# An encoder trunk on one core: values of all heads in one Strassen product, ticks kept out of the edge k tiles, and two `w_out` strips made ahead

## The chip, the core and the metric

The kernel runs on one core of one Trainium2 chip. The metric is the device time of one execution in microseconds, as the median of several runs. Engines: PE is TensorE (matrix products; PEld its weight loads), DVE VectorE, ACT ScalarE, POOL GpSimd, SP SyncE, which issues most DMAs. Accumulators lie in eight PSUM banks of 128x512 float32.

## The reference

Two layers on 256 tokens of width 2048, batch 1, float32. In each layer:

```
u = rmsnorm(x) * g
c_q, c_kv, k_pe, q_na, k_na, v_na, gate_a, gate_b = split(u @ w_in)
y_a = latent_attention(c_q, c_kv, k_pe) @ w_o_mla           # 8 heads, low-rank q and kv, rotary key
y_b = neighbourhood_attention(q_na, k_na, v_na) @ w_o_na    # 8 heads of 128, 2-D window, learned bias
x = x + (sigmoid(gate_a) * y_a + sigmoid(gate_b) * y_b) @ w_out
x = x + square(relu(rmsnorm(x) @ w_ff1)) @ w_ff2            # width 8192 in the middle
```

A last RMSNorm follows. Both attentions are softmax over all 256 keys, the second with a window mask.

## The kernel before, in words

**Two halves of a number.** Matmuls take a rounded float32 form (`F32R`). To keep float32 accuracy each operand is split into a rounded part `hi` and a remainder `lo`, and a product is the three matmuls hi·hi, lo·hi and hi·lo. For weights `parts` (line 172) or `weights` (line 180) make the two: ACT casts `hi`, DVE subtracts to get `lo`. Such a pair of tiles is called a strip here. Activations are split in the same way into tiles called `pair`.

**The product helpers.** All of them load weights by a DMA on SP's queue into `raw` (three buffers of 1 MB), make strips in a ring of four, and issue matmuls.
- `gemm_b` (line 347) has weights as the stationary side and gives transposed results in four banks: for each two k tiles 8 matmuls of 512 columns (L354) and 8 of 256 (L359). It makes queries, keys and latents.
- `gemm_a` (line 325, with `group_a` above it) has activations stationary: 12 matmuls of 512 columns for each two k tiles (L306, L310). The values of four heads, `w_o_na` and `w_o_mla` are made so.
- `gemm_s` (line 524) is partly Strassen, over 1024 output columns and row pairs `j` of two k tiles. A plain row pair takes 8 products, that is 24 matmuls; a Strassen pair takes 7, that is 21 (all L537). For a Strassen pair DVE first makes sums of weight blocks (L574 to L578), and the activations need their own sums, called forms (`forms`, line 479). `order` gives the order of the row pairs; in the layer's first half and for `w_out` it is 0, 4, 1, 5, 2, 6, 3, 7, with 1, 2, 3 as Strassen pairs. Before its first Strassen pair `gemm_s` drains all pending small work (`drain`). At its end one copy and eight additions gather the results from eight banks (L586, L587). The gates, `w_out`, `w_ff1` and `w_ff2` use it.

**Small work between products.** Heads, norms, transposes (`turned`) and forms are generators. `tick` (line 128), called by the products between matmuls, advances one of them, or starts a queued head if six ticks have passed; a generator says how many ticks it sleeps. `have` forces work whose result is needed now. In `gemm_b` a tick stands behind every second `hi` matmul. A head (`na_head`, `mla_head`) computes scores, then `softmax_pv` (line 647): maximum, exponential, reciprocal, scaling of the two probability tiles by the reciprocal (L664, on DVE), 13 ticks later the transposes (L669), 3 ticks later the product with the values.

**The order of the program.** The code gives a program order, and a scheduler that simulates the engines moves instructions within each engine; tiles and pools carry the waits. Layer 0 starts with the queries of all eight neighbourhood heads (`gemm_first`), then for each group of four heads: keys, values, and the four heads are queued. In layer 1 each group also makes its queries. Then come the two latent products, the rotary key, gates and `w_o_na`, the eight latent heads, the rest of `w_o_na`, four column blocks of `w_o_mla`, then `w_out`, and the MLP.

**Pools.** The first half of a layer holds strips of 1024 columns in `wpool` and small tiles of the heads in `tmp`; both belong to `half_a`, which closes behind `w_o_mla`. Then `half_b` opens `wpool2` in that space, with strips of 2048 columns (`strips = True`), and `w_out` begins. `slots` is a ring of 51 tiles of 128x512 for activations of all kinds.

Of the kernel before, what the change touches and what calls it, by code (L numbers as in the profile page):

```python
# [33 lines left out]
F32 = mybir.dt.float32  # L34
F32R = mybir.dt.float32r
# [4 lines left out]
P = 128  # L40
# [35 lines left out]
def trunk(ctx: ExitStack, tc: tile.TileContext, x, x_turned, w_in, w_uq, w_ukv, rpb, w_o_mla, w_o_na,  # L76
# [9 lines left out]
    hbufs, smalls, strips = HBUFS, SMALL, False  # L86

    def bank():
        return psum.tile([P, 512], F32, tag="bank", name="bank", bufs=8)
# [82 lines left out]
    def parts(src):  # L172

        lo, hi = (wpool.tile([P, 2048 if strips else 1024], F32R, tag=tag, name=tag,
                             bufs=hbufs)[:, :src.shape[-1]] for tag in ("lo", "hi"))
        nc.scalar.copy(hi, src)  # L176
        nc.vector.tensor_tensor(lo, src, hi.bitcast(F32), op=ALU.subtract)  # L177
        return hi, lo
# [345 lines left out]
    def gemm_s(w, c0, get, order, pairs, evac):  # L524
# [23 lines left out]
        def cut(src):  # L548
            out, step = [], 2048 if strips else 1024
            for c in range(0, src.shape[-1], step):  # L550
                hi, lo = parts(src[:, c:min(c + step, src.shape[-1])])
                out += [(hi[:, i:i + 512], lo[:, i:i + 512]) for i in range(0, hi.shape[-1], 512)]
            return out

        first = next(j for j in order if j in pairs)
        for j in order:
            raw = raws.tile([P, 2048], F32, tag="raw", name="raw", bufs=RBUFS)
            nc.sync.dma_start(raw.rearrange("p (k n) -> p k n", n=1024),
                              w[2 * j * P:(2 * j + 2) * P, c0:c0 + 1024].rearrange("(k p) n -> p k n", p=P))
            if j not in pairs:  # L560
                ws = cut(raw)
# [85 lines left out]
    def softmax_pv(s, scale, vt, j, put):  # L647
# [15 lines left out]
        for b in range(2):  # L663
            nc.vector.tensor_scalar_mul(p[:, b], p[:, b], inv[:, b:b + 1])  # L664
# [87 lines left out]
    for l in range(DEPTH):  # L752
# [3 lines left out]
        tmp = half_a.enter_context(tc.tile_pool(name="tmp", bufs=2, reuse_waits="tile"))  # L756
# [11 lines left out]
        att_na, ke = [None] * HEADS, [None] * 2  # L768
        for g in range(2):
            qn, kn = (qn[4:] if l == 0 and g else [None] * 4), [None] * 4  # L770
            if l == g == 0:
                qn = [None] * 8
                gemm_first(wi, C_QN, xg, xf4, to_pair(None, qn), squared)
                gemm_b(wi, C_KN, xg, to_pair(mix, kn), scaled, weights(wi, NC, C_KN, 512, tc.keep_in_program_order))
                tables()
            else:
                if l == 0:
                    for t in range(2):
                        tc.keep_in_program_order(nc.sync.dma_start(xt[t], x[t * P:(t + 1) * P]))
                else:  # L780
                    gemm_b(wi, C_QN + g * 512, xg, to_pair(None, qn), scaled if g == 0 else None)
                gemm_b(wi, C_KN + g * 512, xg, to_pair(mix, kn))
# [5 lines left out]
            for j in range(4):  # L788
                h = g * 4 + j
                queued.append(na_head(l, h, qn[j], kn[j], vt, mix.query, setter(att_na, h)))  # L790
# [26 lines left out]
        xs4 = [None] * (NC // 2)  # L817
        start(forms(xf4, MIXED, xs4), 10)
# [25 lines left out]
        mixed = blocks(xg, xs4, MIXED)  # L844
# [53 lines left out]
        mg, ms4, mf4 = [None] * NC, [None] * (NC // 2), [None] * (NC // 2)  # L898
        for c4 in range(4):
# [14 lines left out]
        half_b = ExitStack()  # L914
        strips = True
        wpool = half_b.enter_context(tc.tile_pool(name="wpool2", bufs=4, reuse_waits="tile"))
        tmp = half_b.enter_context(tc.tile_pool(name="tmp2", bufs=2, reuse_waits="tile"))
# [12 lines left out]
        for g in range(2):  # L930
# [11 lines left out]
            gemm_s(w_out[l], g * 1024, blocks(mg, ms4, MERGED), ORDER, MERGED, residual)  # L942
# [142 lines left out]
```

## Time and profile before

| | |
|---|---|
| median of 3 runs | 2599.27 us (2599.08 to 2599.73) |
| the profiled execution, own time | 2599.52 us |
| its span, first to last instruction | 2597.7 us |
| PE busy | 2585.0 us, 12432 matmuls |
| DVE busy | 2176.4 us |
| ACT busy | 1487.5 us |
| granted TensorE clock | 0.999 |
| HBM traffic | 494.28 MB read, 2.10 MB written |

A row of a timeline gives the start and the length in microseconds, engine, line, operation, tiles (written <- read), shape and count, and in brackets the idle time ahead and what ended it. Consecutive instructions of one kind are merged. A group's row gives the busy time, the mean duration of one in nanoseconds and the idle time ahead. Matmuls are pipelined: one lasts longer than the distance from one start to the next. In the layer's first half stages of layer 0 lie at: first queries and keys up to 74 us, values of group 0 to 96, keys and values of group 1 to 147, latents and rotary key to 206, first gate to 248, latent heads 397 to 460, `w_o_mla` up to 526, `w_out` from 527.

### The profile page before, as it was taken

To read this page: it belongs to the slowest core of one execution; us is meant where nothing else is said; L and a number is where in the kernel's file an instruction comes from. 1 tells how busy PE (TensorE), PEld (TensorE's weight loads), DVE (VectorE), ACT (ScalarE), POOL (GpSimd) and SP (SyncE) were. 2 spreads that over 40 slices of the span, in tenths; PEclk is the share of its full clock that TensorE was granted. 3 is DMA by queue.
4 is the path that set the end of the run, shared out by engine and by line. 5 is a ranking of instruction groups with operands and counts; after the bars stand their busy time and mean duration, and the time that the engine had idled before them with its cause. 6 is when DMAs were issued, how large, how long until landed. Compare 5 with 4: busy or idle time off the path is not lost.

```text
span 2597.7 us, 32260 instructions
## 1 busy us (share of the span) xinstructions
PE 2585.0 (100%) x12432; PEld 2171.9 (84%) x12432; DVE 2176.4 (84%) x2538; ACT 1487.5 (57%) x1732; POOL 98.0 (4%) x118
## 2 busy tenths in 40 slices
PE   9999999999999999999999999999999999999998
PEld 8888889888888888888888888898888888888887
DVE  7778889699988898888667788896999988988885
ACT  6555557456655645546545555574666556555463
POOL 0200000000000010000001000000000000100000
PEclk9999999999999999999999999999999999999999
DMA  7655564555577585675565555645656765856754
GB/s 266 217 171 195 180 205 151 165 191 195 195 219 220 176 259 198 202 239 171 178 201 178 173 194 182 205 149 161 197 180 211 234 199 192 246 194 209 243 180 145
DMA packets 173994, 511.06 MB, mean 197 GB/s; under 512 B 13840, under 2 KB 18832, under 8 KB 173584
## 3 DMA queue, kind: packets, MB, share of 16 engines
q1 hardware_dynamic: 164640, 491.78, 57.1%
q0 software_dynamic: 8768, 16.78, 3.3%
q8 instruction: 97, 1.59, 0.2%
q10 hardware_dynamic: 432, 0.43, 0.1%
q14 instruction: 57, 0.47, 0.1%
HBM read 494.28 MB, written 2.10 MB: 191 GB/s over the span
## 4 chain that ended last, share of the span: by engine, by line
PE 99%; issue 0%; ACT 0%; DVE 0%; POOL 0%; DVEq 0%; POOLq 0%; ACTq 0%
PE bank L537 67%; PE bank L306 8%; PE bank L354 6%; PE bank L310 4%; PE bank L359 3%; PE bank L285 2%; PE bank L507 1%; PE bank L260 1%; PE bank L286 1%; PE bank L314 1%; PE bank L316 1%; PE bank L315 1%; PE bank L258 1%; PE bank L669 1%; PE bank L605 0%
## 5 line engine op out<-in xcount | busy, mean ns | idle before, releaser
L537 PE MATMUL bank<-hi,pair 128*128 128x512 f32 x5124 | 1283.4, 390 | 2.1 <-ACT hi L176 2.1
L537 PEld LDWEIGHTS bank<-hi,pair 128*128 128x128 f32 x5124 | 958.0, 188 | 202.5 <-ACT hi L176 2.9
L176 ACT CAST hi<-raw 128x2048 fp32r<-128x2048 f32 (+3 forms) x416 | 622.7, 1517 | 301.7 <-PE bank L537 165.3
L177 DVE TENSOR_TENSOR lo<-raw,hi 128x2048 fp32r<-128x2048 f32 (+3 forms) x416 | 741.6, 1796 | 63.8 <-ACT hi L176 42.2
L537 PE MATMUL bank<-lo,pair 128*128 128x512 f32 x2562 | 697.2, 390 | 0.0
L537 PEld LDWEIGHTS bank<-lo,pair 128*128 128x128 f32 x2562 | 479.7, 188 | 99.4
L176 ACT CAST hi<-sums 128x2048 fp32r<-128x2048 f32 (+1 forms) x150 | 244.9, 1638 | 297.5 <-DVE sums L578 168.9
L177 DVE TENSOR_TENSOR lo<-sums,hi 128x2048 fp32r<-128x2048 f32 (+1 forms) x150 | 290.7, 1948 | 101.2 <-ACT hi L176 58.2
L198 DVE TENSOR_TENSOR lo<-raw,hi 128x1024 fp32r<-128x1024 f32 (+1 forms) x208 | 248.8, 1201 | 102.9 <-ACT hi L197 99.5
L197 ACT CAST hi<-raw 128x1024 fp32r<-128x1024 f32 (+1 forms) x208 | 214.1, 1035 | 205.0 <-PE bank L306 87.6
L306 PE MATMUL bank<-hi,pair 128*128 128x512 f32 x960 | 245.2, 392 | 0.0
L586 DVE TENSOR_TENSOR wide<-wide,bank 128x512 f32<-128x512 f32 x336 | 214.9, 679 | 6.5 <-PE bank L537 6.4
L306 PEld LDWEIGHTS bank<-hi,pair 128*128 128x128 f32 x960 | 178.3, 188 | 35.8
L354 PE MATMUL bank<-pair,hi 128*128 128x512 f32 x640 | 168.8, 395 | 0.0
L574 DVE TENSOR_TENSOR sums<-raw 128x1024 f32<-128x1024 f32 x126 | 153.7, 1220 | 13.9 <-DMA raw<-in_w_ff 7.3
L310 PE MATMUL bank<-lo,pair 128*128 128x512 f32 x480 | 131.9, 391 | 0.0
L354 PEld LDWEIGHTS bank<-pair,hi 128*128 128x128 f32 x640 | 112.4, 189 | 17.7
L310 PEld LDWEIGHTS bank<-lo,pair 128*128 128x128 f32 x480 | 89.4, 188 | 18.0
L516 ACT CAST pair<-wide 128x512 fp32r<-128x512 f32 x110 | 68.2, 620 | 59.8 <-DVE wide L475 57.5
L359 PEld LDWEIGHTS bank<-pair,lo 128*128 128x128 f32 x640 | 89.4, 190 | 7.2
L359 PE MATMUL bank<-pair,lo 128*128 128x256 f32 x640 | 93.7, 283 | 0.0
L578 DVE TENSOR_TENSOR sums<-raw,sums 128x512 f32<-128x512 f32 x126 | 86.6, 687 | 2.0
(165 smaller groups left out, 1890.7 us busy)
## 6 DMA issues: line engine op xcount, KB each, us to landing
raw<-in_w_ff SPq DMA_DIRECT2D x256, 1024.0 KB, 5.4
raw<-in_w_in SPq DMA_DIRECT2D x120, 1024.0 KB, 5.1
raw<-in_w_out SPq DMA_DIRECT2D x32, 1024.0 KB, 5.6
raw<-in_w_o_na SPq DMA_DIRECT2D x16, 1024.0 KB, 5.0
raw<-in_w_o_mla SPq DMA_DIRECT2D x16, 1024.0 KB, 5.0
xt<-wide POOLq DMA_DIRECT2D x48, 256.0 KB, 5.3
raw<-in_w_in SPq DMA_DIRECT2D x17, 512.0 KB, 5.6
raw<-in_w_ukv SPq DMA_DIRECT2D x8, 1024.0 KB, 5.0
```

The lines of the kernel that those rows point to most:

```text
L176: nc.scalar.copy(hi, src)
L177: nc.vector.tensor_tensor(lo, src, hi.bitcast(F32), op=ALU.subtract)
L197: nc.scalar.copy(hi, src)
L198: nc.vector.tensor_tensor(lo, src, hi.bitcast(F32), op=ALU.subtract)
L306: nc.tensor.matmul(ps[t], a, wh[:, k], start=k0 + k + i == 0, stop=False)
L310: nc.tensor.matmul(ps[t], sides(have(acts, k0 + k), t)[0], wl[:, k], start=False, stop=k0 + k == nk - 1)
L354: nc.tensor.matmul(ps[m], wh[:, k, m * P:(m + 1) * P], have(acts, k0 + k), start=k0 + k == 0, stop=False)
L359: nc.tensor.matmul(ps[m][:, :S], wl[:, k, m * P:(m + 1) * P], have(acts, k0 + k)[:, :S], start=False, stop=k0 + k == nk - 1)
L537: nc.tensor.matmul(b[i], x, y, start=count[i] == 1, stop=count[i] == total[i])
L574: nc.vector.tensor_tensor(ts[0].rearrange("p (a n) -> p a n", a=2), raw[:, :512].rearrange("p (a n) -> p a n", a=1).to_broadcast([P, 2, 512]),
L578: final = nc.vector.tensor_tensor(t4, raw[:, 1536:], t2, op=ALU.subtract)
L586: add = lambda o, a, c: nc.vector.tensor_tensor(o, a, c, op=ALU.add)
```

## The change

Five edits.

1. **Values.** One `gemm_s` over all 1024 value columns takes the place of two products of `gemm_a`'s kind (issued in the main body by `group_a`). The forms of x, made so far during the first latent product, are made ahead of it. The results reach `values` from gathered tiles instead of from banks. The first four heads are queued behind it.
2. **Ticks.** `gemm_b` calls no tick in the first two and the last two k tiles.
3. **Softmax scaling** goes from DVE to ACT.
4. **Strips ahead.** During the last column block of `w_o_mla`, a generator closes `tmp`, opens a pool `wpool3` in its space and makes the strips of `w_out`'s row pairs 0 and 4 there. `gemm_s` takes them from `made`. Strips of 2048 columns now alternate, two and two, between `wpool3` and `wpool2` with two buffers each.
5. **Order.** Each such strip's cast and subtraction may not pass the previous strip's on its engine (a dependency without a semaphore).

```diff
@@ parts
+        if strips:
+            whole_strips[0] += 1
+        pool, n, bufs = (stores[whole_strips[0] // 2 % 2], 2048, 2) if strips else (wpool, 1024, HBUFS)
...
+        if strips:
+            for ins, last in zip(made, previous):
+                tc.add_manual_dep(ins.ins, last, ...)
+            previous[:] = [ins.ins.name for ins in made]
@@ gemm_b
-                    if m % 2:
+                    if m % 2 and 0 < k0 < nk - 2:
                         tick()
@@ gemm_s
-            raw = raws.tile([P, 2048], F32, tag="raw", name="raw", bufs=RBUFS)
-            nc.sync.dma_start(...)
+            raw = None if j in made else two_rows(w, c0, j)
             if j not in pairs:
-                ws = cut(raw)
+                ws = made[j] if j in made else cut(raw)
@@ softmax_pv
-            nc.vector.tensor_scalar_mul(p[:, b], p[:, b], inv[:, b:b + 1])
+            nc.scalar.activation(p[:, b], p[:, b], AF.Copy, scale=inv[:, b:b + 1])
@@ main body, first half of a layer
+        if l == 0:
+            gemm_first(wi, C_QN, xg, xf4, to_pair(None, qn), squared)
+            start(forms(xf4, MIXED, xs4), 8)
+            gemm_b(wi, C_KN, xg, put(mix, kn, 0), scaled, weights(...))
+            tables()
+        else:
+            start(forms(xf4, MIXED, xs4), 4)
+            gemm_b(wi, C_QN, xg, put(None, qn, 0), scaled)
+            gemm_b(wi, C_KN, xg, put(mix, kn, 0))
+        mixed, vt = blocks(xg, xs4, MIXED), []
+        gemm_s(wi, C_VN, mixed, ORDER, MIXED, lambda r: vt.extend(values_of(r)))
...
         for g in range(2):
-            ps = [bank() for _ in range(2)]
-            for k0, wh, wl in weights(wi, NC, C_VN + g * 512, 512):
-                group_a(ps, xg, k0, NC, wh, wl)
-                tick()
-            vt = [values(ps[t], mix.col, t) for t in range(2)]
+            if g:
+                if l:
+                    gemm_b(wi, C_QN + 512, xg, put(None, qn, 1))
+                gemm_b(wi, C_KN + 512, xg, put(mix, kn, 1))
...
@@ main body, w_o_mla and w_out
+        def strips_ahead(...):
+            nonlocal strips
+            heads_end.close()
+            stores[0] = half_b.enter_context(tc.tile_pool(name="wpool3", bufs=2, side="right",
+                                                          reuse_waits="tile"))
+            whole_strips[0] = -1
+            for j in ORDER[:2]:
+                strips = True
+                made[j] = cut(two_rows(w_out[l], 0, j))
+                strips = False
...
+                yield 1
...
+            if c4 == 3:
+                start(strips_ahead(), 7)
             gemm_a(w_o_mla[l], c4 * 512, att, merge)
...
+        while len(made) < 2:
+            tick()
         half_a.close()
...
-            gemm_s(w_out[l], g * 1024, blocks(mg, ms4, MERGED), ORDER, MERGED, residual)
+            gemm_s(w_out[l], g * 1024, blocks(mg, ms4, MERGED), ORDER, MERGED, residual, {} if g else made)
```

The line numbers of the new kernel differ: L306, L310, L354, L359, L537 become L313, L317, L361, L366, L557; the strip lines L176 and L177 are both L179, and L197, L198 are L204, L205.

What stands in a row on each engine shows where instructions went. First PE in layer 0, from the end of the values to the next key product. Before, the end of the values of group 0 (L306, L310), the keys of group 1 (L354) and the first head's scores (L314 to L316):

```order
L306 MATMUL bank<-hi,pair 128x512 x8
L310 MATMUL bank<-lo,pair 128x512 x4
L354 MATMUL bank<-pair,hi 128x512 x2
L314 MATMUL bank<-pair 128x256
L315 MATMUL bank<-pair 128x256
L316 MATMUL bank<-pair 128x256
```

Now the last plain row pair of the values (L557) and the same key product (L361, L366):

```order
L557 MATMUL bank<-hi,pair 128x512 x16
L557 MATMUL bank<-lo,pair 128x512 x4
L361 MATMUL bank<-pair,hi 128x512
L557 MATMUL bank<-lo,pair 128x512 x4
L361 MATMUL bank<-pair,hi 128x512
L366 MATMUL bank<-pair,lo 128x256 x2
L361 MATMUL bank<-pair,hi 128x512 x4
L366 MATMUL bank<-pair,lo 128x256 x2
```

The `group_a` rows have gone, the key product takes its banks one by one, and the first scores stand behind its first two k tiles instead of behind two matmuls.

Second, ACT in layer 0 around the start of `w_out`. Before, the last two casts of `w_o_mla` weights are L197, then come four splits of merged activations (L165), and then the strips of `w_out` (L176):

```order
L197 CAST hi_5091<-raw_5064 128x1024
L165 ACTIVATE pair_5039<-bank_5034 128x256
L165 ACTIVATE pair_5042<-bank_5034 128x256
L165 ACTIVATE pair_5054<-bank_5049 128x256
L165 ACTIVATE pair_5057<-bank_5049 128x256
L176 CAST hi_5123<-raw_5120 128x2048
L176 CAST hi_5177<-raw_5174 128x2048
```

Now L204 are the casts of `w_o_mla` and L179 those of `w_out`:

```order
L204 CAST hi_5073<-raw_5055 128x1024
L179 CAST hi_5140<-raw_5138 128x2048
L622 ACTIVATE wide_4984<-bank_4979 128x256 x2
L166 ACTIVATE pair_4987<-wide_4984 128x256
L204 CAST hi_5113<-raw_5111 128x1024
L166 ACTIVATE pair_4990<-wide_4984 128x256
L622 ACTIVATE wide_5002<-bank_4997 128x256 x2
L166 ACTIVATE pair_5005<-wide_5002 128x256
L166 ACTIVATE pair_5008<-wide_5002 128x256
L204 CAST hi_5155<-raw_5111 128x1024
L179 CAST hi_5151<-raw_5149 128x2048
L179 CAST hi_5278<-raw_5272 128x1536
```

The first strip moved ahead of the last two `w_o_mla` casts, the second stands right behind them, and the splits follow.

Third, DVE in layer 0 in the same place, up to the forms of the first Strassen pair of `w_out`. Before, L473 to L476 sum the blocks, L485 makes the remainder of the form, L177 are strips, L574 and L577 sums of weights:

```order
L474 TENSOR_TENSOR wide_5074<-wide_5074,wide_4853 128x128
L169 SCALAR_TENSOR_TENSOR pair_5057<-bank_5049,pair_5057 128x256
L902 SCALAR_TENSOR_TENSOR wide_3666<-wide_3666,bank_5006 128x512
L475 TENSOR_TENSOR wide_5074<-wide_4853,wide_5074 128x128
L902 SCALAR_TENSOR_TENSOR wide_3669<-wide_3669,bank_5007 128x512
L574 TENSOR_TENSOR sums_5226<-raw_5224 128x1024
L903 TENSOR_TENSOR wide_3012<-wide_3012,wide_3666 128x512
L903 TENSOR_TENSOR wide_3015<-wide_3015,wide_3669 128x512
L177 TENSOR_TENSOR lo_5122<-raw_5120,hi_5123 128x2048
L577 TENSOR_TENSOR sums_5226<-raw_5224,sums_5226 128x512
L177 TENSOR_TENSOR lo_5176<-raw_5174,hi_5177 128x2048
L485 TENSOR_TENSOR pair_5080<-wide_5074,pair_5079 128x512
```

Now L480 to L483 sum the blocks, L492 makes the remainder, L179 are strips, and L585 to L589 sums of weights (5272 is the first Strassen pair's `raw`, 5341 the second's):

```order
L179 TENSOR_TENSOR lo_5283<-sums_5274,hi_5282 128x2048
L480 TENSOR_TENSOR wide_5121<-wide_4900 128x128
L483 TENSOR_TENSOR wide_5121<-wide_4900 128x128
L179 TENSOR_TENSOR lo_5314<-raw_5311,hi_5313 128x2048
L170 SCALAR_TENSOR_TENSOR pair_5104<-bank_5096,pair_5104 128x256
L585 TENSOR_TENSOR sums_5343<-raw_5341 128x1024
L481 TENSOR_TENSOR wide_5121<-wide_5121,wide_4900 128x128
L588 TENSOR_TENSOR sums_5343<-raw_5341,sums_5343 128x512
L482 TENSOR_TENSOR wide_5121<-wide_4900,wide_5121 128x128
L589 TENSOR_TENSOR sums_5343<-raw_5341,sums_5343 128x512
L179 TENSOR_TENSOR lo_5348<-raw_5341,hi_5347 128x1536
L492 TENSOR_TENSOR pair_5127<-wide_5121,pair_5126 128x512
```

The form stood behind two strips of plain row pairs; it now stands behind the strips of the first Strassen pair, of the plain pair after it, and of a part of the second Strassen pair. PE's order follows: it takes of the first Strassen pair only the products that need no form, then the next plain pair, and only then the rest. The list from the end of `w_o_mla` to this form has 23 instructions; ahead of the rows shown stand, from L934 on, two multiplications and two additions that merge the last block, three sums of weights, three splits (L170) and one strip of 1536 columns.

More of the change, by code (lines that the diff above doesn't have):

```diff
@@ L86, in trunk @@
     hbufs, smalls, strips = HBUFS, SMALL, False
+    stores, whole_strips, previous = [None, None], [-1], []
     def bank():
@@ L172, in parts @@
     def parts(src):
[L174 to L177, printed above, removed]
+        if strips:
+            whole_strips[0] += 1
+        pool, n, bufs = (stores[whole_strips[0] // 2 % 2], 2048, 2) if strips else (wpool, 1024, HBUFS)
+        hi, lo = (pool.tile([P, n], F32R, tag=tag, name=tag, bufs=bufs)[:, :src.shape[-1]] for tag in ("hi", "lo"))
+        made = nc.scalar.copy(hi, src), nc.vector.tensor_tensor(lo, src, hi.bitcast(F32), op=ALU.subtract)
+        if strips:
+            for ins, last in zip(made, previous):
+                tc.add_manual_dep(ins.ins, last, mybir.DependencyInfo(mybir.DependencyClass.NoSync,
+                                                                      mybir.DependencyReason.DATA))
+            previous[:] = [ins.ins.name for ins in made]
         return hi, lo
@@ L522, in turned_pair, with cut, two_rows, gemm_s @@
         yield
-    def gemm_s(w, c0, get, order, pairs, evac):
+    def cut(src):
+        out, step = [], 2048 if strips else 1024
+        for c in range(0, src.shape[-1], step):
+            hi, lo = parts(src[:, c:min(c + step, src.shape[-1])])
+            out += [(hi[:, i:i + 512], lo[:, i:i + 512]) for i in range(0, hi.shape[-1], 512)]
+        return out
+    def two_rows(w, c0, j):
+        raw = raws.tile([P, 2048], F32, tag="raw", name="raw", bufs=RBUFS)
+        nc.sync.dma_start(raw.rearrange("p (k n) -> p k n", n=1024),
+                          w[2 * j * P:(2 * j + 2) * P, c0:c0 + 1024].rearrange("(k p) n -> p k n", p=P))
+        return raw
+    def gemm_s(w, c0, get, order, pairs, evac, made={}):
         b, count, total = {}, {}, {i: 0 for i in range(1, 9)}
@@ new lines, in trunk, with put, values_of @@
+        qn, kn, xs4 = [None] * 8, [None] * 8, [None] * (NC // 2)
+        def put(norm, dst, g):
+            evac = to_pair(norm, dst)
+            return lambda m, ps: evac(g * 4 + m, ps)
+        def values_of(r):
+            return [[values(r[t, g], mix.col, t) for t in range(2)] for g in range(2)]
+        if l == 0:
+            gemm_first(wi, C_QN, xg, xf4, to_pair(None, qn), squared)
+            start(forms(xf4, MIXED, xs4), 8)
+            gemm_b(wi, C_KN, xg, put(mix, kn, 0), scaled, weights(wi, NC, C_KN, 512, tc.keep_in_program_order))
+            tables()
[3 more added lines that the diff above has]
+            gemm_b(wi, C_KN, xg, put(mix, kn, 0))
@@ new lines, in trunk @@
+        mixed, vt = blocks(xg, xs4, MIXED), []
+        gemm_s(wi, C_VN, mixed, ORDER, MIXED, lambda r: vt.extend(values_of(r)))
+        if l == 0:
+            for t in range(2):
+                tc.keep_in_program_order(nc.sync.dma_start(xt[t], x[t * P:(t + 1) * P]))
+        for g in range(2):
+            if g:
+                if l:
+                    gemm_b(wi, C_QN + 512, xg, put(None, qn, 1))
+                gemm_b(wi, C_KN + 512, xg, put(mix, kn, 1))
+            for h in range(g * 4, g * 4 + 4):
+                queued.append(na_head(l, h, qn[h], kn[h], vt[g], mix.query, setter(att_na, h)))
@@ L898, in trunk, with strips_ahead @@
         mg, ms4, mf4 = [None] * NC, [None] * (NC // 2), [None] * (NC // 2)
+        half_b, made = ExitStack(), {}
+        def strips_ahead(l=l, made=made, half_b=half_b, heads_end=heads_end):
+            nonlocal strips
[7 more added lines that the diff above has]
+                strips = False
+                if j == ORDER[0]:
+                    stores[0].tile([P, 56], F32, name="phase", bufs=1)
+                yield 1
         for c4 in range(4):
@@ L909, in trunk @@
                 start(forms(mf4, MERGED, ms4), 4)
+        while len(made) < 2:
+            tick()
         half_a.close()
         last = l == DEPTH - 1
-        half_b = ExitStack()
         strips = True
-        wpool = half_b.enter_context(tc.tile_pool(name="wpool2", bufs=4, reuse_waits="tile"))
-        tmp = half_b.enter_context(tc.tile_pool(name="tmp2", bufs=2, reuse_waits="tile"))
+        wpool = stores[1] = half_b.enter_context(tc.tile_pool(name="wpool2", bufs=2, reuse_waits="tile"))
         mlp = RowNorm()
```

30 lines of the change are left out of this document (2 added, 28 removed).

## The prediction

> **What bounds the kernel now.** I began with the page: engine totals and the chain of work that ended last.
>
> ```profile
> span 2597.7 us, 32260 instructions
> PE 2585.0 (100%) x12432; PEld 2171.9 (84%) x12432; DVE 2176.4 (84%) x2538; ACT 1487.5 (57%) x1732; POOL 98.0 (4%) x118
> ...
> PE 99%; issue 0%; ACT 0%; DVE 0%; POOL 0%; DVEq 0%; POOLq 0%; ACTq 0%
> ```
>
> The chain is TensorE (PE) throughout. So an edit pays only if it removes matmuls or a PE wait, and costs only if it makes PE wait. The list of PE's waits has only four lines. The longest (total, times, longest one):
>
> ```profile
> PE bank L537 <- ACT hi L176: 2.1, 2, 1.0
> ```
>
> It occurs twice, once a layer, and the other three lie in stages that the change leaves alone. The timeline of PE and ScalarE (ACT) puts it in layer 0 where `w_o_mla` ends (L310) and the product with `w_out` begins (L537):
>
> ```profile
> 525.26 1.07 PE L310 MATMUL bank<-lo,pair 128*128 128x512 f32 x4
> 527.37 3.95 PE L537 MATMUL bank<-hi,pair 128*128 128x512 f32 x16 [1.04 <-ACT hi L176]
> ```
>
> ```profile
> 513.65 1.06 ACT L197 CAST hi<-raw 128x1024 fp32r<-128x1024 f32 x1
> 523.06 0.38 ACT L165 ACTIVATE pair<-bank 128x256 fp32r<-128x256 f32 x1 [8.35 <-PE bank L605]
> ...
> 525.42 3.71 ACT L176 CAST hi<-raw 128x2048 fp32r<-128x2048 f32 x2
> ```
>
> ACT stood idle 8.35 us, then made the first `w_out` strip (L176) when the pool of the first half had closed. A matmul of 512 columns starts every 0.227 us here: four take 1.07, the last one alone its 0.39 of the groups below, so (1.07 - 0.39) / 3 = 0.227. PE could have gone on at 525.26 + 4 x 0.227 = 526.17 and went on at 527.37: 1.20 us late, in two layers 2.40.
>
> Last, the load of each engine by stretch:
>
> ```profile
> core 0: us, PE busy (x) PEld busy (x) DVE busy (x) ACT busy (x) POOL busy (x), PEclk, DMA share, GB/s
> 74.00:96.00 22.00, 22.00 (x101) 18.27 (x100) 14.41 (x20) 11.19 (x17) 1.38 (x1) 1.00 0.84 289
> 96.00:125.00 29.00, 29.00 (x187) 26.10 (x186) 22.88 (x40) 17.09 (x34) 10.01 (x12) 1.00 0.58 183
> 147.00:198.00 51.00, 51.00 (x315) 45.53 (x314) 42.00 (x83) 30.94 (x58) 5.81 (x7) 1.00 0.50 156
> 206.00:248.00 42.00, 42.00 (x187) 34.76 (x186) 35.22 (x44) 24.17 (x29) 0.00 (x0) 1.00 0.59 205
> 397.00:460.00 63.00, 62.73 (x419) 57.39 (x418) 58.19 (x131) 45.19 (x104) 0.00 (x0) 1.00 0.45 145
> 519.00:525.00 6.00, 6.00 (x32) 5.02 (x31) 1.07 (x3) 1.04 (x3) 0.00 (x0) 1.00 0.38 149
> 526.00:560.00 34.00, 32.96 (x150) 27.10 (x149) 33.91 (x40) 20.85 (x18) 0.00 (x0) 1.00 0.60 189
> ```
>
> These are: values of the first four heads; the second key product with four heads; the two latent products with four heads; a Strassen gate product; the eight latent heads with their products; the end of `w_o_mla`; the start of `w_out`. VectorE (DVE) is full in the last, and at 92% among the latent heads, the one other row with PE not full.
>
> **The values product.** Before, each of two groups in two layers takes 8 k steps of 12 matmuls: 4 x 96 = 384. After, each layer has one `gemm_s` with five plain row pairs of 24 and three Strassen pairs of 21: 183, together 366. That is 18 fewer. All are 128x512, of these forms:
>
> ```profile
> L306 PE MATMUL bank<-hi,pair 128*128 128x512 f32 x960 | 245.2, 392 | 0.0
> L537 PE MATMUL bank<-hi,pair 128*128 128x512 f32 x5124 | 1283.4, 390 | 2.1 <-ACT hi L176 2.1
> ```
>
> They last the same in either helper, so each goes at the pitch: 18 x 0.227 = 4.09 us. "TensorE: Matmul & The Clock Gate" of the Trainium skill (section "Wait — 56ns, not 53.3ns?") gives 215.7 ns between matmuls of 512 columns with a warm array, which would make the sum 3.88, an estimate; this trace shows 227, and it decides.
>
> The new helper adds work off PE: DVE subtractions for three pairs, and 16 additions with 2 copies when results are gathered. The gate product at 206 to 248 is the same work at the same size, DVE 35.22 of 42 us, and PE stayed full: taken at nothing. At its end the last additions hold banks that the key product wants; the gate product's end lies inside that same full window, so again 0, with up to 0.5 us a layer as the bad end. The forms of x move ahead of the product (in layer 0 into the first key product, in layer 1 into the first query product), a few microseconds of DVE where the 74 to 96 row shows 7.6 us free in 22: 0.
>
> **Heads.** The first four heads now follow the whole values product. In layer 0 the eight run in the second key product and the two latent ones, which carried four and four before (22.88 of 29 us and 42.00 of 51 of DVE): no denser. With the first and last k tiles free of ticks they start later and closer. 0, and plus or minus 0.5 us.
>
> **Softmax scaling** moves to ACT:
>
> ```profile
> L664 DVE TENSOR_SCALAR p<-p,inv 128x256 f32<-128x256 f32 x64 | 23.1, 404 | 0.6
> L165 ACT ACTIVATE pair<-wide,half 128x256 fp32r<-128x256 f32 x4 | 1.8, 501 | 0.0
> ```
>
> DVE loses 64 x 0.404 = 25.9 us; ACT gains about 64 x 0.501 = 32.1, the price of its nearest row of that size with a scale per partition. In the head windows ACT has 12 of 29 and 20 of 51 us free, and among the latent heads 18 of 63: eight heads x 2 x 0.5 = 8 us fit in either place, and DVE goes from 58.2 to 51.7 of 63 there. PE idles 0.27 us in that row, so no more than 0.3 a layer is to be had. I take 0; PE would wait if a probability tile came later than its transposes, 13 ticks on, which the bad end above covers.
>
> **Two strips ahead.** Two casts and two subtractions of 2048 columns move into the last `w_o_mla` product, where from 519 to 525 DVE is busy 1.07 us and ACT 1.04 of 6. PE can then begin `w_out` at once: -2.40 us, and 0 if another wait takes its place. On ACT the first cast now stands ahead of two smaller ones that `w_o_mla` needs, and would hold them if its load were late. The loads keep their places in SP's queue, and they come early:
>
> ```profile
> 504.09 39.29 SPq L558 DMA_DIRECT2D raw<-in_w_out  x7
> ...
> raw<-in_w_out SPq DMA_DIRECT2D x32, 1024.0 KB, 5.6
> ```
>
> The first lands near 504.1 + 5.6 = 509.7, about when ACT gets there, and the two smaller casts have the 8.35 us of idle time in hand. DVE's full stretch from 526 loses two 2048-column subtractions. This may also shorten short pauses in the first `w_ff1` product:
>
> ```profile
> 635.46 1.14 PE L537 MATMUL bank<-hi,pair 128*128 128x512 f32 x3
> ...
> 637.40 0.40 PE L537 MATMUL bank<-lo,pair 128*128 128x512 f32 x1
> ```
>
> From 635.46 to 637.40 six matmuls should take 1.36 us and take 1.94: 0.6 a layer, 1.2 in all. I take 0 and keep -1.2 as an end. Forcing the strips into program order costs nothing where ACT is half idle, and the two stores of two buffers alternate as one ring of four did: 0.
>
> **The sum.** 4.09 + 2.40 = 6.5 us. The profiled execution took 2599.5 us (span 2597.7 and 1.8 around it), so 2593.0; the median of the runs is 0.25 lower, so 2592.8. A difference of 0.2%, 5.2 us, is about what a measurement of this kernel can tell from no change, so faster means below 2594.1. The ends: 1.2 us more gain gives 2591.6; the small bad ends (two of 0.5 in each of two layers, 2.0) give 2594.8.
>
> **Rivals.** *The wait moves on.* In the new order DVE makes the forms of `w_out`'s first Strassen pair (L492) late: the subtraction just ahead of it already belongs to the second such pair. DVE's list from the end of `w_o_mla`:
>
> ```profile
> L177 DVE TENSOR_TENSOR lo<-raw,hi 128x2048 fp32r<-128x2048 f32 x186 | 423.7, 2286 | 48.0 <-ACT hi L176 35.3 <-PE bank L537 12.3
> L177 DVE TENSOR_TENSOR lo<-raw,hi 128x1536 fp32r<-128x1536 f32 x102 | 178.5, 1750 | 0.0
> L574 DVE TENSOR_TENSOR sums<-raw 128x1024 f32<-128x1024 f32 x126 | 153.7, 1220 | 13.9 <-DMA raw<-in_w_ff 7.3 <-DMA raw<-in_w_in 5.7 <-DMA raw<-in_w_out 0.4
> L577 DVE TENSOR_TENSOR sums<-raw,sums 128x512 f32<-128x512 f32 x126 | 86.3, 685 | 0.8
> L167 DVE TENSOR_TENSOR pair<-wide,pair 128x256 fp32r<-128x256 f32 x18 | 6.8, 419 | 3.5 <-ACT pair L165 3.5
> L473 DVE TENSOR_TENSOR wide<-wide 128x128 f32<-128x128 f32 x42 | 12.0, 285 | 2.7 <-ACT wide L980 2.6
> ...
> 531.15 1.04 PE L605 MATMUL bank<-ident,wide 128*128 128x128 f32 x8
> ```
>
> Strips 2.29 + 2.29 + 2 x 1.75, two of 1024 columns 2.44, nine of 512 columns 6.17 (four of them sums, four merges, the form itself), four of 256 columns 1.68, four of 128 columns 1.14: 19.5 us. PE reaches that form after 83 matmuls and 14 transposes (eight of them 1.04 us, so 0.11 apiece): 18.8 + 1.5 = 20.3 us. So 0.8 us of pauses on DVE is free, and beyond that PE waits. If it waits what it waited before, 2.40 comes back: 2599.27 - 4.1 = 2595.2, no change. For it: DVE full from 526 to 560. Against: the same row holds the two strips that leave. Chance 13%.
>
> *Heads crowd DVE.* If eight heads in layer 0 wait on DVE as the larger of my bad ends, or the evacuation of the values does, some 2 us return: 2594.8, no change. 8%.
>
> *The slots run out.* The ring has 51 slots. At the evacuation of the first latent product of layer 0 stand 16 x pairs, 6 forms, 8 value tiles, 3 held, 4 latents, and for eight heads 16 q and k tiles; each finished head gives back 2 and takes 1. That is 53 minus the finished heads, so it decides if fewer than two have finished: then evacuation waits for a head. A head runs from its first scores to its output:
>
> ```profile
> 97.17 0.28 PE L316 MATMUL bank<-pair 128*128 128x256 f32 x1
> ...
> 114.55 0.41 DVE L167 TENSOR_TENSOR pair<-bank,pair 128x256 fp32r<-128x256 f32 x1
> ```
>
> That is 17.8 us, and PE idle for it gives 2610.6, slower. Against it: four heads start in the key product ahead, 29 us long before. 4%.
>
> **How the numbers follow.** The forecast has 75%: 18 matmuls less and the `w_out` wait gone, 2592.8, itself 2591.6 to 2594.0. The two middle rivals, 21%, are within 0.2%; the slots 4%. So faster 0.75, same 0.21, slower 0.04. A range from 2591.0 (1.2 us in `w_ff1` and 0.6 among the latent heads) to 2595.3 (the wait moved on) leaves out the slots and the tails.
>
> **What would show it.** In the new profile: 366 `gemm_s` matmuls replace 384; no PE wait at the first `w_out` matmul; no new line among PE's waits; ACT busy up by about 32 us, DVE down by less than that. A PE wait on a form pair in `w_out`, on a bank after the values, or on q and k in the latent products would make it wrong, as would a pitch other than 0.227.

## The result and the profile after

The changed kernel takes 2634.3 us (median of 4 runs, 2632.4 to 2634.6); the kernel before, on the same chip, 2599.5 us. The ratio is 1.0132, with a 95% interval of 1.0115 to 1.015: slower by 34.8 us, where 2592.8 us had been forecast. The busy times on the page of after:

```profile
span 2632.3 us, 32248 instructions
PE 2594.2 (99%) x12414; PEld 2169.6 (82%) x12414; DVE 2193.6 (83%) x2520; ACT 1521.5 (58%) x1810; POOL 96.5 (4%) x118
...
PE 93%; DVE 3%; ACT 2%; issue 1%; DMA 0%; POOL 0%; DVEq 0%; POOLq 0%; ACTq 0%
L557 PE MATMUL bank<-hi,pair 128*128 128x512 f32 x5368 | 1343.2, 391 | 23.9 <-ACT hi L179 14.7
```

The 18 matmuls are gone (12414 for 12432). But the chain, 99% PE before, is 93% now, and DVE and ACT stand on it. The group of the Strassen matmuls (L557, which was L537) had 2.1 us of idle time ahead of it and has 23.9. The list of PE's waits of after, where one line of 2.1 us had mattered before:

```profile
PE bank L557 <- ACT hi L179: 14.7, 18, 1.1
PE bank L557 <- ACT wide L960: 6.5, 3, 3.2
PE bank L557 <- DVE lo L179: 2.3, 5, 0.8
...
PE bank L557 <- ACT wide L1014: 1.4, 1, 1.4
PE bank L321 <- ACT pp L682: 1.3, 2, 0.7
PE bank L557 <- DVE pair L170: 1.0, 2, 0.5
```

Eighteen waits for a strip's cast (L179): in each layer four in `w_out`, one in the first product with `w_ff1`, and four behind it, where the forecast had not looked at all. There PE now stops for 1.1 us once in each of the four blocks of the MLP, in the first product with `w_ff2`, 171 us apart. One of these stops on PE's timeline:

```profile
739.22 0.61 PE L557 MATMUL bank<-hi,pair 128*128 128x512 f32 x2
739.67 0.39 PE L557 MATMUL bank<-lo,pair 128*128 128x512 f32 x1
741.15 4.37 PE L557 MATMUL bank<-hi,pair 128*128 128x512 f32 x18 [1.09 <-ACT hi L179]
```

and the same moment on ACT's:

```profile
739.19 3.28 ACT L179 CAST hi<-raw 128x2048 fp32r<-128x2048 f32 x2 [0.63 <-PE bank L557]
742.38 1.91 ACT L179 CAST hi<-sums 128x2048 fp32r<-128x2048 f32 x1
```

ACT was idle and waited for PE: the cast could start only when PE had read the last of what lay in the buffer. A cast takes 1.9 us, and PE came to the new strip after 1.1 us. So each engine waits for the other, and what is short is a buffer.

The two longest stops, 3.2 us in the first product with `w_ff1` in each layer, are not of this kind. PE waits there for transposed x, which ACT brings out of a bank (L960):

```profile
648.57 1.22 PE L557 MATMUL bank<-hi,pair 128*128 128x512 f32 x2 [3.17 <-ACT wide L960]
```

and on ACT that stands behind the cast of a form (L523), which waited for a sum on DVE (L482):

```profile
647.16 0.62 ACT L523 CAST pair<-wide 128x512 fp32r<-128x512 f32 x1 [4.00 <-DVE wide L482]
647.68 0.83 ACT L960 ACTIVATE wide<-bank,g_sb 128x256 f32<-128x256 f32 x2
```

DVE had worked without a pause since 639.88 us. Here the order of the work on ACT and DVE is what holds PE up.

The stop that the forecast wanted to remove is removed. At the start of `w_out` in after the matmuls follow the transposes without a pause:

```profile
524.28 0.82 PE L616 MATMUL bank<-ident,wide 128*128 128x128 f32 x6
524.86 3.89 PE L557 MATMUL bank<-hi,pair 128*128 128x512 f32 x16
```

For the comparisons below, PE's lost time is added up from each trace: for every matmul the time to the start of the next one, less 0.227 us (512 columns), 0.120 (256) or 0.109 (128), both layers together. This table sets the runs side by side, in us; "rest" is everything ahead of `w_out`, the heads and the start of the kernel included:

```
kernel                             rest  w_out 1st  w_out 2nd  w_ff1 1st  MLP after it   sum
before                             10.0     2.6        0.1        1.3         0.8       14.8
after                              12.5     6.5        6.4       15.0        13.1       53.5
after, no forced order             12.9     5.6        3.4       16.8        10.4       49.1
after, edits 1 to 3 alone          14.0     2.6        0.1        1.4         0.2       18.3
after, no strips ahead             12.6     6.5        5.8       15.0        13.1       53.0
after, one pool from w_out's 2nd   12.5     6.5        8.1        5.2         0.2       32.5
 ... and stores by release         13.0     2.2        6.6        3.4         0.2       25.4
after, stores from a list          12.6     2.2        0.0        4.0         0.5       19.3
 ... without forced order          13.5     2.2        0.0        3.2         1.2       20.1
edits 1 and 3 (ticks everywhere)   18.2     2.6        0.1        1.4         0.2       22.5
```

From before to after the sum grows by 38.7 us. Less the 18 matmuls (4.1) that is 34.6, the difference of the spans, 2632.3 - 2597.7.

### The profile page after: what moved, and what is told of

Same layout as the page of the kernel before. It is cut to its first block, busy times and chain, and to the rows that moved or that the text cites. A ratio compares the mean times of both kernels' runs of the same rounds, so it can differ in the third digit from the quotient of the medians.

```text
span 2632.3 us, 32248 instructions
## 1 busy us (share of the span) xinstructions
PE 2594.2 (99%) x12414; PEld 2169.6 (82%) x12414; DVE 2193.6 (83%) x2520; ACT 1521.5 (58%) x1810; POOL 96.5 (4%) x118
## 4 chain that ended last, share of the span: by engine, by line
PE 93%; DVE 3%; ACT 2%; issue 1%; DMA 0%; POOL 0%; DVEq 0%; POOLq 0%; ACTq 0%
PE bank L557 65%; PE bank L313 6%; PE bank L361 6%; PE bank L317 3%; PE bank L366 3%; ACT hi L179 2%; PE bank L292 2%; PE bank L267 1%; PE bank L514 1%; DVE lo L179 1%; PE bank L293 1%; PE bank L321 1%; PE bank L323 1%; PE bank L322 1%; PE bank L265 1%
## 5 line engine op out<-in xcount | busy, mean ns | idle before, releaser
L557 PE MATMUL bank<-hi,pair 128*128 128x512 f32 x5368 | 1343.2, 391 | 23.9 <-ACT hi L179 14.7
L557 PEld LDWEIGHTS bank<-hi,pair 128*128 128x128 f32 x5368 | 1004.7, 188 | 244.0 <-ACT hi L179 23.6
L179 ACT CAST hi<-raw 128x2048 fp32r<-128x2048 f32 (+1 forms) x448 | 652.9, 1477 | 407.6 <-PE bank L557 234.7
L179 DVE TENSOR_TENSOR lo<-raw,hi 128x2048 fp32r<-128x2048 f32 (+1 forms) x448 | 779.1, 1752 | 121.9 <-ACT hi L179 89.3
L557 PE MATMUL bank<-lo,pair 128*128 128x512 f32 x2684 | 724.6, 391 | 2.3 <-DVE lo L179 2.3
L557 PEld LDWEIGHTS bank<-lo,pair 128*128 128x128 f32 x2684 | 502.7, 188 | 108.1 <-DVE lo L179 4.8
L179 ACT CAST hi<-sums 128x2048 fp32r<-128x2048 f32 (+1 forms) x162 | 257.5, 1594 | 270.4 <-DVE sums L589 144.0
L179 DVE TENSOR_TENSOR lo<-sums,hi 128x2048 fp32r<-128x2048 f32 (+1 forms) x162 | 305.2, 1894 | 102.5 <-PE bank L557 54.7
L205 DVE TENSOR_TENSOR lo<-raw,hi 128x1024 fp32r<-128x1024 f32 (+1 forms) x176 | 211.8, 1214 | 58.1 <-ACT hi L204 49.3
L204 ACT CAST hi<-raw 128x1024 fp32r<-128x1024 f32 (+1 forms) x176 | 180.1, 1031 | 119.8 <-PE bank L313 47.4
L597 DVE TENSOR_TENSOR wide<-wide,bank 128x512 f32<-128x512 f32 x352 | 225.4, 680 | 8.4 <-PE bank L557 8.3
L313 PE MATMUL bank<-hi,pair 128*128 128x512 f32 x704 | 180.6, 393 | 0.0
L585 DVE TENSOR_TENSOR sums<-raw 128x1024 f32<-128x1024 f32 x132 | 161.1, 1220 | 14.5 <-DMA raw<-in_w_ff 5.2
L361 PE MATMUL bank<-pair,hi 128*128 128x512 f32 x640 | 170.4, 394 | 0.0
L313 PEld LDWEIGHTS bank<-hi,pair 128*128 128x128 f32 x704 | 130.6, 188 | 26.0
L361 PEld LDWEIGHTS bank<-pair,hi 128*128 128x128 f32 x640 | 111.6, 189 | 16.6
L523 ACT CAST pair<-wide 128x512 fp32r<-128x512 f32 x110 | 68.3, 621 | 63.7 <-DVE wide L482 61.5
L366 PEld LDWEIGHTS bank<-pair,lo 128*128 128x128 f32 x640 | 92.7, 190 | 9.1
L366 PE MATMUL bank<-pair,lo 128*128 128x256 f32 x640 | 98.8, 284 | 0.0
L317 PE MATMUL bank<-lo,pair 128*128 128x512 f32 x352 | 96.7, 392 | 0.0
L589 DVE TENSOR_TENSOR sums<-raw,sums 128x512 f32<-128x512 f32 x132 | 90.7, 687 | 1.7
L588 DVE TENSOR_TENSOR sums<-raw,sums 128x512 f32<-128x512 f32 x132 | 90.5, 686 | 0.9
```

Source lines behind the costliest of these rows:

```text
L179: made = nc.scalar.copy(hi, src), nc.vector.tensor_tensor(lo, src, hi.bitcast(F32), op=ALU.subtract)
L313: nc.tensor.matmul(ps[t], a, wh[:, k], start=k0 + k + i == 0, stop=False)
L317: nc.tensor.matmul(ps[t], sides(have(acts, k0 + k), t)[0], wl[:, k], start=False, stop=k0 + k == nk - 1)
L557: nc.tensor.matmul(b[i], x, y, start=count[i] == 1, stop=count[i] == total[i])
L585: nc.vector.tensor_tensor(ts[0].rearrange("p (a n) -> p a n", a=2), raw[:, :512].rearrange("p (a n) -> p a n", a=1).to_broadcast([P, 2, 512]),
L588: nc.vector.tensor_tensor(t2, raw[:, 1024:1536], t1, op=ALU.subtract)
```

## The experiments

The theory after the two traces: the two stores of two buffers (edit 4) are not the pool of four that they replace. The rivals: the forced order (edit 5), the values with their heads (edits 1 to 3), and the making ahead itself.

**1. After, without the forced order.**

```diff
-            for ins, last in zip(made, previous):
-                tc.add_manual_dep(ins.ins, last, ...)
```

> The changed kernel without edit 5: casts and subtractions of the strips are no longer held in program order; the two stores of two buffers stay. Theory A (the forced order costs the 34.8 us): the time falls to the 2592 to 2598 us of the blind sum. Theory B (the two stores cost it: a strip must wait for a buffer of its own store although one of the other store is free): most of the loss stays, 2610 to 2640 us, and ACT hi and DVE lo stay the releasers of PE's waits in the MLP. Theory C (values, ticks or the softmax scaling cost it): no change, 2634 us.

2629.2 us, ratio to before 1.0114 (1.0099 to 1.0129). Order alone is not it. It may be a small part: the time is 5.1 us shorter than that of the change, but the two intervals overlap. Most of the loss stays, and the waits change their names; of PE's waits:

```profile
PE bank L552 <- ACT hi L179: 7.2, 8, 1.3
PE bank L552 <- DVE lo L179: 6.9, 5, 2.6
PE bank L552 <- ACT pair L518: 3.5, 10, 0.4
```

**2. Edits 1 to 3 alone.** One pool of four again, nothing made ahead:

```diff
-        pool, n, bufs = (stores[whole_strips[0] // 2 % 2], 2048, 2) if strips else (wpool, 1024, HBUFS)
+        pool, n, bufs = (wpool, 2048, HBUFS) if strips else (wpool, 1024, HBUFS)
-                start(strips_ahead(), 7)
```

> Edits 1 to 3 alone: values in one Strassen product, ticks kept out of the edge k tiles, softmax scaling on ACT; one pool of four 2048-column buffers as before, nothing made ahead, no forced order. Theories A and B both: 18 matmuls fewer at 0.227 us = 4.1 us less than before, plus the two heads waits of 0.9 us each that are new in the trace of after: 2596 to 2598 us, and no wait of PE in the MLP. Theory C: 2625 us or more.

2597.5 us, 0.9992 (0.9982 to 1.0001). The whole loss is gone, and the two waits at the start of `w_out` (2.1 us) are back:

```profile
PE bank L262 <- ACT hi L246: 2.1, 1, 2.1
PE bank L552 <- ACT hi L179: 2.1, 2, 1.0
...
PE bank L316 <- ACT pp L677: 1.3, 2, 0.7
```

The first line lies at 6 us, before any of the edits, and is not in the other profiles at this size. With one pool the forced order changes nothing at all: built with it and without it, this kernel has the same instructions in the same order on every engine, and so has the kernel before.

**3. Two stores and forced order, but no strips ahead.** Both stores are opened where `w_out` begins.

> The changed kernel with the two stores of two and the forced order, but no strip made ahead: both stores are opened where w_out begins. Theory B: the waits are those of the split stores, so the time stays at 2634 us, plus up to 2.4 us for the two waits at the start of w_out that come back: 2632 to 2638 us. Rival D (it is the making ahead, with its pool on the right and its strips out of turn, that costs): 2596 to 2602 us.

2654.5 us, 1.021 (1.0193 to 1.0227), over 16 us above the higher of the two ranges expected. A window in the MLP without a single wait shows that this is another effect:

```profile
780.00:860.00 80.00, 80.00 (x357) 65.32 (x356) 68.41 (x61) 41.27 (x32) 3.55 (x4) 1.00 0.70 214
```

PE is full at a granted clock of 1.00, but starts 357 matmuls; the run of experiment 4 starts 363 in the same window. Set beside the addresses of the built kernel, the matmuls that read a strip of the first store follow each other at 233.4 ns (3053 of them), all others of that line at 227.5. The changed kernel puts 224 bytes that nobody uses into the first store; I had dropped them with `strips_ahead`, and the first store's strips then began 224 bytes past a multiple of 256. All strips of before and after begin at a multiple.

**4. The same with the 224 bytes put back.**

```diff
+            if g == 0:
+                stores[0].tile([P, 56], F32, name="phase", bufs=1)
```

> As the run with the two stores and the forced order but no strip made ahead (2654.5 us), with the 224 unused bytes of the changed kernel put back into the first store, so that all strips start at multiples of 256 bytes again. In the run without them every matmul that reads a strip of the first store followed its forerunner by 233.4 ns, and by 227.5 where the strip lay in the second. If that is the start address: 3053 matmuls x 6 ns = 18 us less, 2636 us, which is the changed kernel's 2634.3 plus the waits at the start of w_out. If it is the stores or their place on the right: 2654 us.

2634.2 us, 1.0133 (1.0119 to 1.0147). The address was it: the two built kernels have the same instructions in the same order on every engine, and only the first store's strips lie elsewhere, by 224 bytes. The same window now:

```profile
780.00:860.00 80.00, 80.00 (x363) 66.28 (x362) 68.45 (x61) 45.46 (x35) 3.54 (x4) 1.00 0.70 220
```

And two stores without a strip made ahead are as slow as the whole change, so making strips ahead is not what costs. In the table the two differ by 0.5 us in sum.

**5. One pool of four again from the second product of `w_out` on.**

```diff
+            if g:
+                half_b.close()
+                wpool = half_b.enter_context(tc.tile_pool(name="wpool4", bufs=4, reuse_waits="tile"))
+                stores[:], depth[0] = [wpool, wpool], 4
```

> The changed kernel, strips ahead and split stores kept for the first product of w_out alone; before the second product both stores are closed and one pool of four buffers is opened, as in the kernel before. Theory B: the waits of the second product of w_out (5.0 us more than before in both layers), of the first product of w_ff1 (15.2) and of the rest of the MLP (12.7) go, those of the first product of w_out (5.3) stay: 2634.3 - 32.9 = about 2601 us. Theory A: the order is still forced where it has an effect, so 2625 us or more. Theory C: 2634 us.

2614.0 us, 1.0055 (1.004 to 1.007). In the MLP the lost time falls from 13.1 us to 0.2, as expected. But the sum came out 13 us high. Some 5 us of that lie in the first product of `w_ff1`, which still loses 5.2 us; about 7 lie in the second product of `w_out`, where the exchange of pools stops PE itself:

```profile
571.62 3.18 PE L557 MATMUL bank<-hi,pair 128*128 128x512 f32 x12
577.36 2.13 PE L557 MATMUL bank<-lo,pair 128*128 128x512 f32 x8 [2.55 <-DVE lo L179]
```

ACT's casts ahead of it had waited for PE:

```profile
570.85 3.29 ACT L179 CAST hi<-raw 128x2048 fp32r<-128x2048 f32 x2 [6.02 <-PE bank L557]
```

The new pool's buffers lie where other tiles of both stores lay, and in the built kernel its second strip waits for one of the last matmuls of the product before.

**6. As 5, and in `w_out`'s first product each strip goes to the store whose buffer comes free first.** From here on the stores by twos and by release differ only in these digits, for the eleven strips of `w_out`'s first product:

```
the pool of four gives the buffers   a b c d a b c a b a d
stores by twos (the change)          0 0 1 1 0 0 1 1 0 0 1
stores by release (a, b = 0; c, d = 1)  0 0 1 1 0 0 1 0 0 0 1
```

> As the run that opens one pool of four again before the second product of w_out (2614.0 us), but the eleven strips of the first product go to the stores by the order in which their buffers come free (0 0 1 1 0 0 1 0 0 0 1) instead of by twos. Theory B: the waits inside the first product (2.9 us in each layer) go, 2614.0 - 5.8 = 2608 us; the wait where one pool takes the stores' place (2.7 us in each layer, and 1.5 and 0 us of half-rate matmuls behind it) stays, since the new pool's buffers do not lie where the stores' lay. Rival: the waits inside the first product are late DVE forms and not buffers: 2612 to 2614 us.

2609.3 us (2605.7 to 2609.9), 1.0034 (1.0022 to 1.0046): as expected for buffers, not for late forms. The first product's lost time falls from 6.5 to 2.2 us; the stop at the exchange of pools stays, now as `PE bank L557 <- DVE lo L179` (3.4 us) and `PE bank L514 <- DVE xt L970` (2.4).

**7. The change whole, with the store of each strip from a list.** All 195 strips of a layer go where the pool of four would have put them; two stores, strips ahead, forced order, all stay.

```diff
-        ... stores[whole_strips[0] // 2 % 2] ...
+        ... stores[int(STORE[whole_strips[0]])] ...
```

> The changed kernel whole, strips ahead, two stores of two and forced order included; only the store of each strip is not given by counting twos but by a written list, in which each strip goes to the store that holds the buffer which the single pool of four would have given it. Theory B (a strip waits for a buffer of its own store while the other store has a free one): the waits in the second product of w_out and in the MLP go, and the two waits at the start of w_out stay away: 2592 to 2597 us. Rival E (two stores cost in themselves, whichever strip goes where, or the forced order does): 2615 to 2635 us.

2600.1 us, 1.0003 (0.9994 to 1.0013). With nothing but the digits changed, 34.2 us of the 34.8 are back. This is the shortest proof, and the built kernels say how it comes about. Below are the strips around the stop at 739 us in after: the matmul (counted along PE) after which its buffer is free, the first that reads the strip, and the last:

```
strip, store by twos   freed first last      strip, store by list   freed first last
47 sums  1              3494  3571  3628      47 sums  0              3494  3557  3663
50 sums  1              3582  3612  3631      50 sums  0              3590  3609  3666
51 raw   1              3628  3633  3648      51 raw   1              3594  3617  3642
52 raw   0              3594  3649  3662      52 raw   1              3624  3651  3670
53 sums  0              3608  3663  3670      53 sums  1              3642  3657  3673
```

A strip is read over anything from 6 to 107 matmuls in the run with the list (47 over 107, 51 over 26). By twos, strips 47 and 50 hold store 1's two buffers until matmuls 3628 and 3631, and strip 51 must go there: 5 matmuls lie between its buffer's release and its use, 1.1 us for a cast of 1.9. Store 0 had had two free buffers since matmuls 3594 and 3608. Such a gap of 5 occurs 12 times in after, six times a layer: in the first products of `w_out` and of `w_ff1`, and in the first `w_ff2` product of each block. Twelve stops stand at these places; with the matmul behind each they make some 15 of the 53.5 us that after loses. In `w_out`'s second product the smallest gaps are 8 matmuls. In before the smallest gap is 14 matmuls, 3.2 us. Strip 51, for which ACT waits in after (739.19 above), ACT casts in this run without a pause, 4.0 us before PE starts on it at 724.74:

```profile
720.74 1.91 ACT L181 CAST hi<-raw 128x2048 fp32r<-128x2048 f32 x1
```

What PE still waits for in it:

```profile
PE bank L559 <- ACT hi L181: 1.5, 2, 0.8
...
PE bank L323 <- ACT pp L684: 1.3, 2, 0.7
PE bank L559 <- DVE lo L181: 0.8, 2, 0.4
PE bank L559 <- ACT pair L525: 0.7, 2, 0.4
PE bank L323 <- ACT pair L168: 0.5, 2, 0.3
PE bank L559 <- ACT wide L962: 0.5, 2, 0.2
```

The two long stops for transposed x (L960, now L962) are down to 0.2 us each. In after they and the slow matmuls right behind them lose some 9 us. Since only the digits differ, the stores by twos bring them about, but by way of the order on ACT and DVE, and no run shows that link by itself.

**8. As 7, without the forced order.**

> As the run with the written list of stores (2600.1 us), without the forced order of casts and subtractions. If the order costs something where the stores fit (the waits of 0.9 us in the first product of w_out and of 1.7 us where w_ff1 begins, in each layer): 2595 to 2598 us. If it costs nothing, as the forecast had it: 2600 us.

2600.45 us, 1.0002 (0.9993 to 1.0011): where the stores fit, the order costs nothing that can be told.

**9. Edits 1 and 2 alone (softmax scaling back on DVE).**

```diff
-            nc.scalar.activation(p[:, b], p[:, b], AF.Copy, scale=inv[:, b:b + 1])
+            nc.vector.tensor_scalar_mul(p[:, b], p[:, b], inv[:, b:b + 1])
```

> Edits 1 and 2 alone: as the run of edits 1 to 3 (2597.5 us), with the softmax scaling back on DVE. If the two waits of the local heads for ACT pp (0.9 and 0.8 us, new with the change) come from the scaling, which ACT now does between its exponentials and the copy, they go: 1.7 us less, 2595.8 us. If they come from where the heads' steps stand in the program, they stay: 2597.5 us.

2599.2 us, 0.9999 (0.9989 to 1.001). The waits for ACT pp stay, and there is one more:

```profile
PE bank L316 <- ACT pp L677: 2.1, 3, 0.8
```

So the scaling did not make them. Against the run of edits 1 to 3 (2597.5) the intervals overlap: edit 3 is worth nothing that these runs can tell.

**10. Edits 1 and 3 alone (a tick in every k tile again).**

```diff
-                    if m % 2 and 0 < k0 < nk - 2:
+                    if m % 2:
```

> Edits 1 and 3 alone: as the run of edits 1 to 3 (2597.5 us), with a tick again in every k tile of the products. If the two waits of the local heads for ACT pp (0.9 and 0.8 us) come from ticks that fall closer together because the edge k tiles have none, they go: 2595.8 us. Blind theory, that edit 2 costs and gains nothing: 2597.5 us.

2604.3 us, 1.0019 (1.0008 to 1.0029), against both expectations. New waits of the heads appear:

```profile
PE bank L317 <- DVE pp L678: 2.3, 2, 1.1
...
PE bank L675 <- ACT p L670: 1.0, 2, 0.6
PE bank L356 <- DVE small L324: 0.7, 1, 0.7
```

These waits read as if DVE's steps came late for PE when eight heads follow one another and also run at the edges of a product; that reading was not tried further. Its interval lies above that of edits 1 to 3.

**11. Edit 2 alone, in the kernel before.**

> Edit 2 alone: the kernel before, with no tick in the first and last two k tiles of the products. The forecast gave this edit nothing: 2599.5 us. Rival, from the run of edits 1 and 3 without edit 2 (2604.3 against 2597.5 us): if holding the heads out of the edges gains by itself, 2593 us; if it only repairs what the heads' new neighbours cost, 2599.5 us.

2600.45 us, 1.0000 (0.9991 to 1.0009). Alone it is worth nothing, so in the change it repairs what edit 1 costs.

**12. Edits 1 to 3, and one tick more between a head's transposes and its last product.**

```diff
-SPACING, LAG1, LAG2 = 6, 13, 3
+SPACING, LAG1, LAG2 = 6, 13, 4
```

> As the run of edits 1 to 3 (2597.5 us), with 4 ticks instead of 3 between a head's transposes and its product with the values, so that ACT has longer for the copy that PE waited for. If the two waits for ACT pp (0.9 and 0.8 us) are a head's lag that is one tick short: 1.7 us less, 2595.8 us. If the later product only pushes the next step of the heads late: 2597.5 us or more.

2598.2 us, 0.9992 (0.9983 to 1.0001): a miss. The line `PE bank L316 <- ACT pp L677: 1.3, 2, 0.7` stands unchanged, so the lag is not what brings that wait about. This run and that of edits 1 to 3 are the fastest here; their intervals still touch 1, so neither is shown to beat the kernel before.

## Why the prediction was wrong, step by step

**The 18 matmuls: right.** They are gone, the pitch is 0.227 us where nothing waits, and the spans agree with 4.1 us less work.

**The step that failed** is "the two stores of two buffers alternate as one ring of four did: 0". There was no ring of four. The pool gave each strip the buffer that came free first (a b c d a b c a b a d; in the built kernel before, this holds for every strip of layer 0 behind the first four), which lets short strips pass the long ones; the stores by twos take that away. The term should have been about 34 us: experiment 7, which differs from the change in that alone, is 34.2 us faster. Per stage (after less experiment 7): 4.3 in `w_out`'s first product, 6.4 in its second, 11.0 in the first of `w_ff1` (some 9 us of after's 15.0 there are the two long stops and the slow matmuls right behind them), 12.6 in the rest of the MLP. The forecast priced the edit where it was made, at the start of `w_out`, although it also set the buffers of every strip for the remaining 770 us or so of a layer.

**The `w_out` wait: removed, but little gained.** The term said 2.40 us. With the list of stores, the first product loses 2.2 us where before lost 2.6: another wait has come 24 us later, 0.8 us in each layer (`PE bank L559 <- ACT hi L181: 1.5, 2, 0.8` in experiment 7), for a strip whose buffer comes free only 10 matmuls ahead. That the wait could move on had been a rival, but through DVE's late forms; the place named there cost 1.0 us in after (`DVE pair L170`) and nothing in experiment 7.

**The first product of `w_ff1`: worse, not 0 or better.** With the list it loses 4.0 us for 1.3, on strips and on the transposed x (`ACT pair L525`, `ACT wide L962`). The last twelve transposes of x stand 17 matmuls later in PE's order there than in the kernel of edits 1 to 3. Why the order came out so was not tried, and stays open.

**Heads and softmax: the nothing held only thanks to edit 2.** The heads cost 1.3 us of waits for ACT pp in after, inside the bad end; without edit 2 the kernel of edits 1 to 3 takes 6.8 us longer (experiments 2 and 10). So "heads crowd DVE" was real, and the edit to which I gave no value is what contains it. What makes the remaining wait is open: neither the scaling (9) nor the lag (12). DVE's busy time rose by 17 us instead of falling: the 26 us of scaling left, but the values product brought 16 additions (11 us) and subtractions (16 us), which the forecast had named, and 18 sums of weights (16 us), which it had not named. It cost nothing that shows. Two of the waits that the forecast put into stages left alone (0.3 us each) lie among the latent heads, which edit 3 does touch; they stayed as they were.

**The forced order: right, 0, where the buffers fit** (experiment 8, and the equal programs of experiment 2). With the stores by twos it stays open: without it the time was 5.1 us shorter (experiment 1), with intervals that overlap.

The sum by these measured terms: -4.1 for the matmuls, +34.2 for the stores, and experiment 7's other differences to before (rest +2.6, `w_out` -0.5, `w_ff1` and MLP +2.4) +4.5: 34.6, where 34.8 was measured.

## What to carry to other kernels

A pool that hands out whatever buffer is free is more than its count: splitting it, or fixing who gets which, costs wherever the contents live for different times, and it costs at every later use, not only where the split was made. Before such an edit, list for each tile when its buffer is freed and when the tile is first read, and compare that gap with the time of the instruction that fills it. And when an edit moves one piece, keep the unused bytes around it: the address of an operand can be tuned too.

## What the hardware showed

**A start address that costs 2.6%.** In experiment 3 matmuls of 512 columns took 233.4 ns from start to start when the strip began 224 bytes past a multiple of 256 bytes, 227.5 when it began on one, at a granted clock of 1.00 in both; 224 unused bytes took 20.3 us off the kernel (experiment 4). Other offsets were not tried.

**A pause costs again afterwards.** After the pause of 3.2 us in after's first `w_ff1` product, matmuls start every 0.427 us for some 5 us; the windows ahead of the pause and behind it (granted clock in the column PEclk):

```profile
core 0: us, PE busy (x) PEld busy (x) DVE busy (x) ACT busy (x) POOL busy (x), PEclk, DMA share, GB/s
636.00:645.00 9.00, 8.54 (x34) 5.96 (x33) 8.84 (x14) 5.16 (x8) 2.93 (x1) 1.00 0.62 219
648.50:655.00 6.50, 6.15 (x14) 4.42 (x15) 3.94 (x3) 5.81 (x6) 0.00 (x0) 0.53 0.01 4
655.00:665.00 10.00, 10.00 (x45) 8.26 (x44) 7.81 (x5) 5.98 (x4) 0.00 (x0) 1.00 0.97 321
```

Whether it happens is not a matter of the length alone. In experiment 5 the same pause occurs in both layers, 2.55 us at 574 and 2.58 at 1874. After the first PE went on at 1.00, after the second at 0.66, with seven matmuls 0.427 us apart:

```profile
576.00:582.00 6.00, 4.64 (x20) 3.86 (x21) 6.00 (x7) 0.72 (x2) 0.00 (x0) 1.00 0.58 172
1876.00:1881.00 5.00, 4.75 (x14) 3.79 (x15) 5.00 (x7) 0.72 (x2) 0.00 (x0) 0.66 0.72 211
```

"TensorE: Matmul & The Clock Gate" of the Trainium skill (Part 1) says that a window of about 3.4 us decides on the clock and runs on freely, so that it matters where in it the matmuls fall. That agrees with two equal pauses and two clocks; the 0.427 us fits the 426.7 ns that it gives for half the clock. It does not agree on the length: the Trainium skill there has the clock fall after an idle window of about 3.4 us, and here pauses of 2.58 and 3.2 us were enough.
